# The residual moved to DRAM during the experts, and its SBUF room given to two more weight-chunk places (6 to 8)

## The chip, the cores and the metric

The kernel runs on one core of a Trainium2 chip. The metric is the device time of one execution in microseconds (us); lower is better. The arithmetic is float32 throughout, partly as split pairs of matmuls.

## The reference: one decoder block

512 tokens of width 1024 go through two sub-layers. The first normalises, projects, mixes (eight heads of dilated attention beside four heads of gated linear attention) and projects back. The second is a mixture of 32 experts, four for each token. Both add a gated, normalised result to the residual `x`:

```
x = x + gate1 * rms_norm(hybrid_mixer(h), g_post_mix)     # after this line x is "the residual" of the text
h = rms_norm(x, g_pre_ffn) * (1 + scale2) + shift2
y = moe_ffn(h, router, w_gate_up[32], w_down[32], ...)    # top 4 of 32 experts, clamped SwiGLU
x = x + gate2 * rms_norm(y, g_post_ffn)                   # the residual is read once more, here
```

An expert's weights are 1024 x 2048 (gate and up) and 1024 x 1024 (down), 12 MiB in float32. All 32 are read whatever the routing: 384 MiB.

## The kernel before

**The stages.** Up to about 366 us the mixer runs, then the router: `post(i, ys)` does it for the token tile i (128 tokens, i from 0 to 3). In it the residual of the tile is formed in place in the SBUF tile `X[:, i, :]` (`X` holds 4 x 4 KiB in each of the 128 partitions); it is transposed for the router, squared for its norm, and scaled into `h2`, which goes to DRAM (`h2_d`). From 366 to about 1540 us the experts run, ordered by how many tokens they have. The last 20 us, the tail, add everything up: `acc_d`, in which the experts have summed their outputs in DRAM, is loaded, normalised, added to `X`, and stored.

**Chunks and places.** An expert's weights come in twelve chunks of 1 MiB (the code's "halves"), 384 in all, loaded by `load_half` on SP's DMA queue. Each chunk lands in one of the places of `ring["wr"]`, which are used in turn: 6 places of 8 KiB a partition before the change (five from the pool `wr`, the sixth, `wr6`, opened a little later). The chunks 6 to 8 go once to three extra places, the pool `wx`, which is closed after them. A place is free again when its chunk has been used: for an expert with over 64 tokens in a block, ACT rounds the chunk (`ehi`) and DVE takes the rest (`elo`), in `split_e`, and then the place is free, while PE works from `ehi` and `elo`; for a block of up to 64 tokens ("narrow") PE reads the chunk itself (`gemm_half`; in the profile `bc<-wr` and `ac<-wr`).

**Lists and gathers.** Before an expert starts, `lists` loads its token numbers from a table in DRAM (`li<-tab`, on SP's queue among the chunks), GpSimd gathers the tokens' rows of `h2_d` (`xg<-h_d`, or `xq<-h_d` for narrow blocks), and PE transposes them (`prep`). Bias rows come in small loads (`cb`, `cc`). Outputs are added into `acc_d` by indirect DMAs that GpSimd issues.

**What sets the order.** Nothing is placed by hand from engine to engine. The kernel records its operations in the class `Order`; `S.run()` then lays them out with a cost for each operation, a DMA model and the number of places of each ring, and emits them in that order on each engine. So the number of places does not only bound what is in flight: it changes the order on every engine. In the engines' queues an instruction waits for its semaphores, and what stands behind it waits too. At the end of the experts stands a loop for overflow blocks (`tc.For_i`, line 1628), before which every engine waits for all DMAs.

Of the kernel before, what the change touches and what calls it, by code (L numbers as in the profile page):

```python
# [11 lines left out]
F32 = mybir.dt.float32  # L12
# [5 lines left out]
OP = mybir.AluOpType  # L18
# [4 lines left out]
P, T, NT, D, KD = 128, 512, 4, 1024, 8  # L23
# [7 lines left out]
FIRST, PREP, WX = 8, 9, 3  # L31
# [243 lines left out]
def tile_hybrid_block(ctx, tc, x, c, w_mod, b_mod, g_pre_mix, w_in, w_gate_lr, b_gate, g_gla, w_out,  # L275
                      g_post_mix, g_pre_ffn, router_w, router_b, w_gate_up, b_gate_up, w_down, b_down,
                      g_post_ffn, ca_d, cb_d, tab_d, out, dbg=None):
    nc = tc.nc
# [18 lines left out]
    def close_pool(name):  # L297
# [6 lines left out]
    dp = ctx.enter_context(tc.tile_pool(name="dp", bufs=1, space=DRAM))  # L304
# [12 lines left out]
    S = Order(NB_, 500, ("s", "tr"))  # L317

    ring = {}
# [14 lines left out]
        nc.tensor.matmul(o, l, r, start=start, stop=stop, **kw)  # L334

    h2_d = dp.tile([T, D], F32, name="h2_d")
    acc_d = dp.tile([T + P, D], F32, name="acc_d")
    tab = dp.tile([E * TR, 4], I32, name="tab")
    mrow = dp.tile([8, 512], F32, name="mrow")
# [17 lines left out]
    X = px.tile([P, NT, D], F32, name="X")  # L357
# [55 lines left out]
    def load(q, byt, fn, r=(), w=()):  # L413
        S.op(q, 1.05 if q == "pool" else 0.1, fn, r=r, w=w, byt=byt)
# [44 lines left out]
    for i in range(NT):  # L459
        load("sp", 1 << 19, lambda i=i: nc.sync.dma_start(X[:, i, :], x[i * P:(i + 1) * P]),  # L460
             w=[f"px/Xl{i}", f"px/Xh{i}"])
# [28 lines left out]
    for i in range(NT):  # L490
        S.op("act", _act(1024), lambda i=i: nc.scalar.activation(
            hC[:, 2 * i:2 * i + 2, :].rearrange("p a c -> p (a c)"), X[:, i, :], AF.Square, accum_out=ss1[:, i:i + 1]),
             r=[f"px/Xl{i}", f"px/Xh{i}"], w=[f"ma/C{2 * i}", f"ma/C{2 * i + 1}", f"cp/ss1{i}"])
    cols = [CRG, CQ, CK, CV, CQKG, CVG]
    raws, sp = {}, {}
# [87 lines left out]
    def proj_k(o, n, i, k):  # L583
# [8 lines left out]
         w=["mx/wlr"])  # L592
    for b in range(2):
# [6 lines left out]
                                                      op0=OP.mult), r=["cp/ca"], w=[wlr2])  # L600
    S.op("act", .2, lambda: nc.scalar.activation(wlr2.t[:, :, 0:16], wlr, AF.Copy), r=["mx/wlr"], w=[wlr2])
    S.op("dve", .25, lambda: nc.vector.tensor_sub(wlr2.t[:, :, 16:32], wlr, wlr2.t[:, :, 0:16].bitcast(F32)),
         r=["mx/wlr"], w=[wlr2])
# [378 lines left out]
    def merge(i):  # L982

        S.stream = "mrg"
        oh, ol = buf("oh", [P, KD, P], F32R), buf("ol", [P, KD, P], F32R)
        oTs[i] = oh, ol
        s = slice(i * P, (i + 1) * P)
        S.op("act", _act(512), lambda: nc.scalar.activation(oh.t[:, 0:4, :], qT[:, :, s], AF.Copy), r=[f"mx/q{i}"],
             w=[oh])
        S.op("dve", _dve(512), lambda: nc.vector.tensor_sub(ol.t[:, 0:4, :], qT[:, :, s], oh.t[:, 0:4, :].bitcast(F32)),  # L990
             r=[f"mx/q{i}", oh], w=[ol])
        pt = bank("tr")

        def tr():
            for h in range(4):
                nc.tensor.transpose(pt.t[:, h * P:(h + 1) * P], vg[:, i, h * P:(h + 1) * P], ident)
        S.op("pe", .44, tr, r=[f"px/Xl{i}", f"mx/q{i}", "cp/ca"], w=[pt])
        pv = lambda: pt.t.rearrange("p (h t) -> p h t", h=4)
        S.op("act", _act(512), lambda: nc.scalar.activation(oh.t[:, 4:8, :], pv(), AF.Copy), r=[pt], w=[oh])
        S.op("dve", _dve(512), lambda: nc.vector.tensor_sub(ol.t[:, 4:8, :], pv(), oh.t[:, 4:8, :].bitcast(F32)),  # L1000
             r=[pt, oh], w=[ol])
        load("sp", 1 << 19, lambda: nc.sync.dma_start(X[:, i, :], x[i * P:(i + 1) * P]),
             w=[f"px/Xl{i}", f"px/Xh{i}"])
# [38 lines left out]
    def post(i, ys):  # L1042
        S.stream = "post"
        v = buf("v", [P, 10])
        xi = X[:, i, :]
# [93 lines left out]
             r=xk + [v, rowsA], w=[hk])  # L1139
        S.op("dve", _dve(1024), lambda: nc.vector.tensor_add(h2(), h2(), rv["sh2"]()), r=[rowsB], w=[hk])  # L1140
        load("sp", 1 << 19, lambda: nc.sync.dma_start(h2_d[i * P:(i + 1) * P], h2()), r=[hk] + hold, w=[f"dp/h2{i}"])

    merge(0)
    for i in range(EARLY, NT):
        gla(i)
# [137 lines left out]
    LI, XG, XT, AT, YS, BS, PRE = {}, {}, {}, {}, {}, {}, {}  # L1283
    C = {}

    def load_half(rk, st, h, tag="wr", r=()):
        b = buf(tag, [P, 4, 512])
        load("sp", 1 << 20, lambda: nc.sync.dma_start(
            b.t.rearrange("p (k a) c -> p k (a c)", a=2),
            wsrc(st[0], reg(rk))[h * 256:h * 256 + 256, st[1] * D:st[1] * D + D].rearrange("(k p) c -> p k c", p=P)),  # L1290
            r=rk_(rk) + list(r), w=[b])
        return b
# [3 lines left out]
    def open_wr(name, n):  # L1296
        p = open_pool(name, "right", reuse_waits="tile")
        ring["wr"] = [p.tile([P, 4, 512], F32, name=f"{name}{i}") for i in range(n)] + ring.get("wr", [])
    o1 = S.open("wr", lambda: open_wr("wr", NB_["wr"][0] - 1), after=[c1])
    BB = []  # L1300

    def load_biases():
        for n, (src, w) in enumerate(((b_gate_up, D), (b_down, 512))):
# [3 lines left out]
                load("sp", 32 * 4 * w, lambda b=b, sv=sv, bf_=bf_: nc.sync.dma_start(  # L1307
                    bf_.t[b * E:(b + 1) * E].rearrange("e (s c) -> e s c", c=512), sv[:, :, b // 2, :]), w=[bf_])
            BB.append((bf_, w))
    for n, q in enumerate(halves[:NB_["wr"][0] + WX]):  # L1310
        PRE[q] = load_half(*q, tag="wr" if n < NB_["wr"][0] else "wx", r=["we/w"] if n >= NB_["wr"][0] - 1 else [])
        if n == NB_["wr"][0] - 2:
            cw = S.close(["w2", "md"], lambda: [close_pool(p) for p in ("md", "w2")])

            def open_we():
                open_wr("wr6", 1)
                open_pool("we", "right", reuse_waits="tile")
                open_pool("wx", "right", reuse_waits="tile")
            o2 = S.open("we", open_we, after=[o1, cw])
            S.opened["wx"] = o2  # L1320
            load_biases()
# [272 lines left out]
    consts_a()  # L1594
    prep(E - 1)
    for n, q in enumerate(halves):
        if n == NB_["wr"][0] + WX:
            cx = S.close(["wx"], lambda: close_pool("wx"))

            def open_t2():  # L1600
                p = open_pool("t2", "left", reuse_waits="tile")
                for tag in ("xh", "xl"):
                    ring[tag].insert(0, p.tile([P, KD, P], F32R, name=f"{tag}2"))
            S.open("t2", open_t2, after=[cx, ot])
        for go, r in ahead.get(n, []):
            if go:
                gather(r)
                prep(r)
            else:
                lists(r)  # L1610
        half(*q)
        if n == len(halves) - 6:
            gpb = buf("xg", [P, D])
            load("pool", 1 << 19, lambda: nc.gpsimd.dma_start(gpb.t, mrow_b(None, 3)), w=[gpb])
# [5 lines left out]
    def pair():  # L1620
        t = ring["wr"].pop()
        return [t[:, 2 * h:2 * h + 2, :].rearrange("p a c -> p (a c)") for h in range(2)]
# [29 lines left out]
        S.run()  # L1652


    yp, zp, sq = pair() + pair(), pair() + pair(), pair()[0]
    for i in range(NT):
        nc.sync.dma_start(yp[i], acc_d[i * P:(i + 1) * P])
    nc.scalar.activation(fv[:, 4:5], fv[:, 5:6], AF.Sqrt)
# [6 lines left out]
    for i in range(NT):  # L1665
        z = zp[i]
        nc.scalar.activation(sq, yp[i], AF.Square, accum_out=fv[:, i:i + 1])
        nc.scalar.activation(fv[:, i:i + 1], fv[:, i:i + 1], AF.Sqrt, scale=1.0 / D, bias=fv[:, 5:6])
        nc.vector.reciprocal(fv[:, i:i + 1], fv[:, i:i + 1])
        nc.vector.scalar_tensor_tensor(z, z, fv[:, i:i + 1], X[:, i, :], op0=OP.mult, op1=OP.add)  # L1670
        nc.sync.dma_start(out[i * P:(i + 1) * P], z)
        if i < 2:
            scaled(i + 2, (nc.vector, nc.gpsimd)[i])
# [25 lines left out]
```

## Time and profile before

| what | value |
|---|---|
| time, median of 3 runs (lowest, highest) | 1585.73 us (1584.68, 1587.38) |
| the profiled execution, its own time | 1577.37 us |
| its span, first to last instruction | 1575.5 us |
| busy over the span: PE, DVE, ACT, POOL | 89%, 50%, 38%, 12% |
| moved by DMA | 487.72 MB, 310 GB/s over the span |
| mean granted TensorE clock | 0.969 of full speed |

All rows of the trace come from the profiled execution, which was 8.36 us faster than the median of the three runs; a difference in microseconds is carried over to the median as it is. The DMA share of a stretch is the mean busy share of the 16 DMA engines; in a full stretch it reads slightly above 1.

### The profile page before, as it was taken

To read this page: it belongs to the slowest core of one execution; us is meant where nothing else is said; L and a number is where in the kernel's file an instruction comes from. 1 tells how busy PE (TensorE), PEld (TensorE's weight loads), DVE (VectorE), ACT (ScalarE), POOL (GpSimd) and SP (SyncE) were. 2 spreads that over 40 slices of the span, in tenths; PEclk is the share of its full clock that TensorE was granted. 3 is DMA by queue.
4 is the path that set the end of the run, shared out by engine and by line. 5 is a ranking of instruction groups with operands and counts; after the bars stand their busy time and mean duration, and the time that the engine had idled before them with its cause. 6 is when DMAs were issued, how large, how long until landed. Compare 5 with 4: busy or idle time off the path is not lost.

```text
span 1575.5 us, 17649 instructions
## 1 busy us (share of the span) xinstructions
PE 1409.0 (89%) x6268; PEld 804.4 (51%) x6268; DVE 782.9 (50%) x1164; ACT 596.9 (38%) x798; POOL 183.1 (12%) x161
## 2 busy tenths in 40 slices
PE   3999999987999899899889999999999899999983
PEld 2777666754656544444445553343454443444551
DVE  5787746676765413131356652232565532223663
ACT  4433534433555412122344452223454532224552
POOL 2331001122101000000020020000211101001002
PEclk9999999998999999999989999999999999999997
DMA  9477601176799999989999999999998989989994
GB/s 349 161 265 241 214 1 59 41 260 223 254 398 359 325 366 353 363 308 379 380 344 379 339 385 387 371 369 358 385 394 322 390 305 383 378 330 390 395 357 124
DMA packets 145754, 487.72 MB, mean 310 GB/s; under 512 B 14800, under 2 KB 15328, under 8 KB 145648
## 3 DMA queue, kind: packets, MB, share of 16 engines
q1 hardware_dynamic: 136048, 461.37, 78.4%
q0 software_dynamic: 9616, 25.19, 6.7%
q8 instruction: 51, 0.84, 0.2%
q14 instruction: 39, 0.32, 0.1%
HBM read 467.39 MB, written 19.46 MB: 309 GB/s over the span
## 4 chain that ended last, share of the span: by engine, by line
PE 69%; DMA 13%; DVE 10%; ACT 4%; issue 2%; SPq 0%; POOL 0%; POOLq 0%; DVEq 0%; ACTq 0%
PE ac L334 30%; PE bc L334 21%; PE pj L334 10%; DMA wr<-in_w_gate_up 9%; ACT ehi L1527 3%; DVE elo L1537 3%; PE s L334 2%; DVE mq L478 2%; PE tx L1393 1%; DMA wr<-in_w_down 1%; PE ms L334 1%; PE tx L1408 1%; DMA raw<-in_w_mod 1%; DMA raw<-in_w_in 1%; DVE gl L1499 1%
## 5 line engine op out<-in xcount | busy, mean ns | idle before, releaser
L1537 DVE TENSOR_TENSOR elo<-wr,ehi 128x2048 fp32r<-128x2048 f32 x165 | 377.5, 2290 | 216.7 <-ACT ehi L1527 176.5
L1527 ACT ACTIVATE ehi<-wr 128x2048 fp32r<-128x2048 f32 x165 | 314.0, 1909 | 152.1 <-DMA wr<-in_w_gate_up 109.8
L334 PE MATMUL bc<-wr,xL 128*64 128x512 f32 x1152 | 275.3, 609 | 1.4 <-DMA wr<-in_w_gate_up 1.4
L334 PE MATMUL ac<-ehi,xh 128*128 128x512 f32 (+2 forms) x480 | 170.1, 416 | 26.0 <-ACT ehi L1527 26.0
L334 PE MATMUL ac<-ehi,xl 128*128 128x512 f32 (+2 forms) x480 | 164.3, 404 | 0.0
L334 PE MATMUL ac<-elo,xh 128*128 128x512 f32 (+2 forms) x480 | 141.9, 409 | 6.3 <-DVE elo L1537 6.2
L334 PEld LDWEIGHTS bc<-wr,xL 128*64 128x64 f32 x1152 | 73.6, 137 | 138.0 <-issue 133.7
L334 PE MATMUL bc<-wr,aL 128*64 128x512 f32 x576 | 137.2, 615 | 3.6 <-DMA wr<-in_w_down 3.6
L334 PEld LDWEIGHTS ac<-ehi,xh 128*128 128x128 f32 (+2 forms) x480 | 83.8, 183 | 75.1 <-ACT ehi L1527 37.9
L334 PEld LDWEIGHTS ac<-elo,xh 128*128 128x128 f32 (+2 forms) x480 | 81.5, 179 | 57.2 <-issue 22.7
L1497 DVE TENSOR_SCALAR gu<-bc 128x256 f32<-128x256 f32 x36 | 15.3, 424 | 188.2 <-ACT gl L1495 148.4
L334 PEld LDWEIGHTS ac<-ehi,xl 128*128 128x128 f32 (+2 forms) x480 | 87.5, 182 | 26.6 <-DVE xl L1398 0.2
L334 PE MATMUL ac<-ehi,ah 128*128 128x512 f32 (+2 forms) x240 | 85.0, 416 | 2.7 <-ACT ehi L1527 2.7
L1474 POOL DMA_INDIRECT acc_d<-yL,li x20 | 38.5, 1923 | 399.7 <-ACT yL L1472 353.2
L334 PE MATMUL ac<-ehi,al 128*128 128x512 f32 (+2 forms) x240 | 81.7, 402 | 0.0
L1495 ACT ACTIVATE gl<-bc 128x256 f32<-128x256 f32 x36 | 13.8, 383 | 179.2 <-PE bc L334 163.8
L334 PE MATMUL pj<-whi,hC 128*128 128x512 f32 x192 | 79.7, 415 | 0.9 <-ACT hC L560 0.9
L334 PE MATMUL pj<-whi,hD 128*128 128x512 f32 x192 | 76.2, 397 | 1.7 <-POOL hD L563 1.7
L334 PEld LDWEIGHTS bc<-wr,aL 128*64 128x64 f32 x576 | 38.2, 139 | 77.2 <-issue 72.1
L334 PE MATMUL pj<-wlo,hC 128*128 128x512 f32 x192 | 76.1, 397 | 0.0
L334 PE MATMUL ac<-elo,ah 128*128 128x512 f32 (+2 forms) x240 | 68.0, 396 | 0.0
L478 DVE SCALAR_TENSOR_TENSOR mq<-raw,sil,mq 128x512 f32<-128x512 f32 x74 | 59.2, 800 | 2.1 <-DMA raw<-in_w_mod 0.4
(336 smaller groups left out, 1683.6 us busy)
## 6 DMA issues: line engine op xcount, KB each, us to landing
wr<-in_w_gate_up SPq DMA_DIRECT2D x254, 1024.0 KB, 10.4
wr<-in_w_down SPq DMA_DIRECT2D x127, 1024.0 KB, 10.8
raw<-in_w_mod SPq DMA_DIRECT2D x21, 1024.0 KB, 6.2
raw<-in_w_in SPq DMA_DIRECT2D x12, 1024.0 KB, 10.9
X<-in_x SPq DMA_DIRECT2D x8, 512.0 KB
raw<-in_w_out SPq DMA_DIRECT2D x4, 1024.0 KB
acc_d<-vt SPq DMA_DIRECT2D x5, 512.0 KB, 10.8
wlo<-in_w_mod SPq DMA_DIRECT2D x2, 1024.0 KB
```

The source lines that it names most:

```text
L334: nc.tensor.matmul(o, l, r, start=start, stop=stop, **kw)
L478: f = lambda k=k, s=s: nc.vector.scalar_tensor_tensor(a.t, t.t[:, k, :], s, a.t, op0=OP.mult, op1=OP.add)
L1393: nc.tensor.transpose(pt.t[:, k * m:(k + 1) * m], src(k), ident[:m, :m])
L1408: nc.tensor.transpose(pt.t[:, k * P:(k + 1) * P], src.t[:, k * P:(k + 1) * P], ident)
L1474: load("pool", 1 << 18, lambda: nc.gpsimd.indirect_dma_start(out=acc_2, out_offset=bass.IndirectOffsetOnAxis(ap=li.t[:, 1:2], axis=0), in_ ...
L1495: S.op("act", _acm(256), lambda: nc.scalar.activation(gl.t[:m], gate(), AF.Gelu_apprx_sigmoid), r=[o], w=[gl], table="g")
L1497: S.op("dve", _dvm(256), lambda: nc.vector.tensor_scalar(gu.t[:m], up(), 8.0, -6.0, op0=OP.min, op1=OP.max), r=[o], w=[gu])
L1499: S.op("dve", _dvm(256), lambda: nc.vector.scalar_tensor_tensor(gl.t[:m], gl.t[:m], C["s7"][:m], gu.t[:m], op0=OP.min, op1=OP.mult), r=[gu ...
L1527: S.op("act", _acm(2048), lambda: nc.scalar.activation(hi.t, raw.t, AF.Copy), r=[raw], w=[hi])
L1537: S.op(eng, _dvm(n) if eng == "dve" else .15 + .0021 * n, lambda e=e, c=slice(c0, c1): e.tensor_tensor(lo.t[:, :, c], raw.t[:, :, c], hi.t ...
```

## The change

Four things are edited. (1) `post` also writes the finished residual of its tile to a DRAM tensor `x1_d`, on SP's queue. (2) As chunk 9 comes up, `open_x` puts two places at the head of the ring that are the rows 0 and 1 and the rows 2 and 3 of `X`; it depends on the four writes (`kept`). The ring then has 8 places, and `Order` plans with 8. (3) The chunks 9 and 10 are loaded ahead of everything else recorded for chunk 9, into these two places. (4) In the tail four loads of 512 KiB bring the residual back from `x1_d`, ahead of the four loads of `acc_d`; the last addition reads them in place of `X`.

```
-           "wr": (6, "wr"), ...
+           "wr": (8, "wr"), ...
+    x1_d = dp.tile([T, D], F32, name="x1_d")
@@ post()
         load("sp", 1 << 19, lambda: nc.sync.dma_start(h2_d[i * P:(i + 1) * P], h2()), r=[hk] + hold, w=[f"dp/h2{i}"])
+        kept.append(S.op("sp", 0.1, lambda: nc.sync.dma_start(x1_d[i * P:(i + 1) * P], xi), r=xk, w=[f"dp/x1{i}"],
+                         byt=1 << 19))
@@
+    def open_x():
+        ring["wr"] = [X[:, 2 * n:2 * n + 2].rearrange("p i (k c) -> p (i k) c", c=512) for n in range(2)] + ring["wr"]
@@
-    o1 = S.open("wr", lambda: open_wr("wr", NB_["wr"][0] - 1), after=[c1])
+    o1 = S.open("wr", lambda: open_wr("wr", 5), after=[c1])
+    nwr = 6
@@ the loop over the chunks
-        if n == NB_["wr"][0] + WX:
+        if n == nwr + WX:
+            S.open("xw", open_x, after=kept)
+        if n in (nwr + WX, nwr + WX + 1):
+            PRE[q] = load_half(*q, r=["xw/w"])
+        if n == nwr + WX:
             cx = S.close(["wx"], lambda: close_pool("wx"))
@@ the tail
-    yp, zp, sq = pair() + pair(), pair() + pair(), pair()[0]
+    yp, zp, xp, sq = pair() + pair(), pair() + pair(), pair() + pair(), pair()[0]
+    for i in range(NT):
+        nc.sync.dma_start(xp[i], x1_d[i * P:(i + 1) * P])
     for i in range(NT):
         nc.sync.dma_start(yp[i], acc_d[i * P:(i + 1) * P])
...
-        nc.vector.scalar_tensor_tensor(z, z, fv[:, i:i + 1], X[:, i, :], op0=OP.mult, op1=OP.add)
+        nc.vector.scalar_tensor_tensor(z, z, fv[:, i:i + 1], xp[i], op0=OP.mult, op1=OP.add)
```

Since `Order` lays the program out anew, three places show what moved. The first is SP, where the experts begin (the profile's 366 us). `wr_...` and `X` are the places that chunks go to, `li<-tab` the token lists, `ISA` a register step for an address. Before, two chunks stand ahead of the first list:

```order
L1288 ISA
L1288 DMA wr_2633<-in_w_gate_up 128x2x1024
L1288 DMA wr_2634<-in_w_down 128x2x1024
L1349 DMA li<-tab 128x4
L1355 ISA
L1355 DMA li<-tab 64x4
```

Now, with the first two of them in `X`:

```order
L1296 ISA
L1296 DMA X<-in_w_gate_up 128x2x1024
L1296 DMA X<-in_w_down 128x2x1024
L1296 ISA
L1296 DMA wr_2636<-in_w_gate_up 128x2x1024
L1296 DMA wr_2637<-in_w_down 128x2x1024
L1316 DMA cb<-in_b_gate_up 32x2x512
L1316 DMA cc<-in_b_down 32x512
L1358 DMA li<-tab 128x4
L1364 ISA
L1364 DMA li<-tab 64x4
```

Four chunks and a pair of bias rows now stand ahead of the first list. The last pair of bias rows, which stood between the lists before, comes later still, behind a fifth chunk.

The second place is PE at the same time: the matmuls of the first expert (`ac<-ehi`, `ac<-elo`, and the bias `ac<-bhl`) around the first transposes of gathered rows (`tx<-ca,xq`). Before:

```order
L334 MATMUL ac<-ehi,xl_2975 128x512 x2
L334 MATMUL ac<-elo,xh_2973 128x512 x2
L334 MATMUL ac<-bhl,bs 128x512
L334 MATMUL ac<-elo,xh_2973 128x512 x2
L334 MATMUL ac<-bhl,bs 128x512
L1408 MATMUL tx<-ca,xq 128x128 x4
L334 MATMUL ac<-elo,xh_2973 128x512 x4
```

Now:

```order
L334 MATMUL ac<-elo,xh_2984 128x512 x4
L334 MATMUL ac<-bhl,bs 128x512 x2
L334 MATMUL ac<-ehi,xh_2984 128x512 x2
L334 MATMUL ac<-ehi,xl_2986 128x512 x2
L334 MATMUL ac<-ehi,xh_2984 128x512 x2
L334 MATMUL ac<-ehi,xl_2986 128x512 x2
L334 MATMUL ac<-elo,xh_2984 128x512 x4
L334 MATMUL ac<-ehi,xh_2984 128x512
L334 MATMUL ac<-ehi,xl_2986 128x512
L334 MATMUL ac<-ehi,xh_2984 128x512
L334 MATMUL ac<-ehi,xl_2986 128x512
L1417 MATMUL tx<-ca,xq 128x128 x4
```

Between the first expert's own transposes and `tx<-ca,xq` PE had 58 matmuls before and has 90 now, the bias ones among them.

The third place is SP at the end, behind the overflow loop. Before:

```order
L1628 REGISTER_ALU
L1628 COMPARE_AND_BRANCH
L1628 UNCONDITIONAL_BRANCH
L1657 DMA wr_2635<-acc_d 128x1024 x2
L1657 DMA wr_2634<-acc_d 128x1024 x2
L1671 DMA out<-wr_2633 128x1024 x2
L1671 DMA out<-wr_2785 128x1024 x2
```

Now:

```order
L1641 REGISTER_ALU
L1641 COMPARE_AND_BRANCH
L1641 UNCONDITIONAL_BRANCH
L1670 DMA wr_2640<-x_d 128x1024 x2
L1670 DMA wr_2639<-x_d 128x1024 x2
L1672 DMA wr_2636<-acc_d 128x1024 x2
L1672 DMA X<-acc_d 128x1024 x2
L1686 DMA out<-X 128x1024 x2
L1686 DMA out<-wr_2789 128x1024 x2
```

The four loads of the residual stand behind the loop and ahead of those of `acc_d`.

## Rows read from the trace of the kernel before

**Rows 1.** The page: DMA share (tenths) and rate in 40 equal slices of the span
```profile
DMA  9477601176799999989999999999998989989994
GB/s 349 161 265 241 214 1 59 41 260 223 254 398 359 325 366 353 363 308 379 380 344 379 339 385 387 371 369 358 385 394 322 390 305 383 378 330 390 395 357 124
```
**Rows 2.** Windows by stage: us, busy PE, PEld, DVE, ACT, POOL; clock, DMA share, GB/s
```profile
300.00:366.00 66.00, 55.05 (x282) 36.93 (x280) 46.35 (x155) 23.60 (x48) 13.11 (x25) 0.92 0.58 193
366.00:430.00 64.00, 57.60 (x252) 41.27 (x252) 44.40 (x52) 33.95 (x33) 11.91 (x7) 0.92 0.76 249
430.00:1530.00 1100.00, 1011.18 (x4318) 522.11 (x4317) 468.99 (x488) 401.28 (x434) 97.63 (x61) 0.98 0.99 365
1030.00:1040.00 10.00, 10.00 (x46) 4.54 (x44) 3.27 (x4) 1.14 (x4) 0.00 (x0) 1.00 1.03 413
```
**Rows 3.** Windows of 2 us in 430:1530 with a DMA share under 0.95
```profile
430.00:432.00 2.00, 2.00 (x9) 1.43 (x8) 1.02 (x1) 1.22 (x2) 0.00 (x0) 1.00 0.92 279
...
678.00:680.00 2.00, 2.00 (x11) 1.70 (x12) 1.77 (x5) 0.85 (x3) 0.00 (x0) 1.00 0.57 225
680.00:682.00 2.00, 2.00 (x13) 0.73 (x11) 1.61 (x5) 0.85 (x3) 0.00 (x0) 1.00 0.02 6
682.00:684.00 2.00, 2.00 (x12) 0.69 (x10) 0.63 (x2) 0.38 (x1) 0.00 (x0) 1.00 0.21 31
684.00:686.00 2.00, 2.00 (x12) 0.58 (x8) 0.00 (x0) 0.00 (x0) 0.00 (x0) 1.00 0.82 330
...
1496.00:1498.00 2.00, 2.00 (x10) 1.45 (x9) 0.94 (x1) 1.89 (x1) 0.00 (x0) 1.00 0.89 307
```
**Rows 4.** Waits of SP's queue in 430:1540: us in total, times, longest
```profile
SPq L1288 <- PE bc L334: 434.4, 180, 9.8
SPq L1288 <- DVE elo L1537: 218.2, 74, 14.5
```
**Rows 5.** Waits in 430:1540, ACT's longest on a DMA and PE's two longest
```profile
ACT ehi L1527 <- DMA wr<-in_w_gate_up: 109.4, 42, 7.7
...
PE ac L334 <- ACT ehi L1527: 28.7, 21, 3.2
PE tx L1393 <- DVE gl L1499: 25.0, 17, 3.8
```
**Rows 6.** The chain that ended last, in 430:1540, by line
```profile
by line: PE ac L334 40.2%; PE bc L334 29.5%; DMA wr<-in_w_gate_up 12.6%; ACT ehi L1527 4.3%; DVE elo L1537 3.7%; issue 2.0%; PE tx L1393 1.8%; PE tx L1408 1.7%; DMA wr<-in_w_down 1.1%; DVE gl L1499 1.0%; DVE gu L1497 0.7%; ACT gl L1495 0.5%
```
**Rows 7.** The chain where the experts begin: start us, us, what
```profile
366.65 9.10 DMA wr<-in_w_down
...
378.11 3.64 DMA li<-tab
...
384.00 7.63 DMA xq<-h_d,li
...
411.50 17.00 PE ac L334 x74
```
**Rows 8.** PE's waits in 384:392: us in total, times, longest
```profile
PE tx L1408 <- DMA xq<-h_d,li: 4.0, 1, 4.0
PE ac L334 <- DVE elo L1537: 1.6, 1, 1.6
```
**Rows 9.** DMA issues of the page: times, KB each, median us to landing
```profile
wr<-in_w_gate_up SPq DMA_DIRECT2D x254, 1024.0 KB, 10.4
li<-tab SPq DMA_DIRECT2D x40, 1.0 KB, 10.6
```
**Rows 10.** The timeline of the tail: start us, us, instruction, wait and releaser
```profile
1556.17 1.78 SPq L1657 DMA_DIRECT2D wr<-acc_d  x4
...
1559.35 1.06 ACT L1667 ACTIVATE wr<-wr 128x1024 f32<-128x1024 f32 x1 [1.55 <-DMA wr<-acc_d]
...
1560.69 2.34 POOL L1661 TENSOR_TENSOR wr<-wr,xg 128x1024 f32<-128x1024 f32 x1 [8.71 <-DMA wr<-acc_d]
1564.82 2.62 POOL L1661 TENSOR_TENSOR wr<-wr,xg 128x1024 f32<-128x1024 f32 x1 [1.80 <-DMA wr<-acc_d]
```

More of the change, by code (lines that the diff above doesn't have):

```diff
@@ L1141, in post @@
         load("sp", 1 << 19, lambda: nc.sync.dma_start(h2_d[i * P:(i + 1) * P], h2()), r=[hk] + hold, w=[f"dp/h2{i}"])
+        kept.append(S.op("sp", 0.1, lambda: nc.sync.dma_start(x1_d[i * P:(i + 1) * P], xi), r=xk, w=[f"dp/x1{i}"],
+                         byt=1 << 19))
+    kept = []
     merge(0)
@@ L1309, in load_biases @@
             BB.append((bf_, w))
-    for n, q in enumerate(halves[:NB_["wr"][0] + WX]):
-        PRE[q] = load_half(*q, tag="wr" if n < NB_["wr"][0] else "wx", r=["we/w"] if n >= NB_["wr"][0] - 1 else [])
-        if n == NB_["wr"][0] - 2:
+    for n, q in enumerate(halves[:nwr + WX]):
+        PRE[q] = load_half(*q, tag="wr" if n < nwr else "wx", r=["we/w"] if n >= 5 else [])
+        if n == 4:
             cw = S.close(["w2", "md"], lambda: [close_pool(p) for p in ("md", "w2")])
```

2 rows, old and new, of the table NB_ are left out of this document.

## The prediction, on record before the changed kernel ran

> **What bounds the kernel now.** I read the page's slices first, to see whether the DMA engines ever rest while the experts run. From the tenth slice on they read 8 or 9 tenths, at 305 to 398 GB/s [rows 1]. So the experts are near the limit of the DMA, and PE is near its own: from 430 to 1530 us PE is busy 1011.2 of 1100 us, and the DMA share is 0.99 [rows 2]. A full stretch reads 1.03, at 413 GB/s (1030 to 1040 us, same group). That makes the time in which the DMA engines rest 1100 x (1.03 - 0.99) / 1.03 = 43 us, or 32 us if full is taken as 1.02.
>
> Where they rest I read from windows of 2 us. Of 550 there are 58 with a share under 0.95 (the first, the last and one complete pause in [rows 3]). What they lack of 1.00 adds up to 35 us. They lie in about fifteen pauses, and the longest lacks 4.8 us: 0.43 + 0.98 + 0.79 + 0.18, times 2 us, at 678 to 686 us. In the pause shown PE is busy all the time. So it is not that nothing is wanted: the chunks are all loaded and none is used up fast enough.
>
> SP's waits say the same. It waits 434.4 us in 180 pieces for PE to finish with a place that a narrow block reads, and 218.2 us in 74 pieces for DVE to finish `elo` [rows 4]. Both are waits for a place, and most cost nothing, since several chunks are still under way meanwhile. They cost when all are down.
>
> The other half of the swing is on ACT and PE: ACT waits 109.4 us in 42 pieces for a chunk to land before it can make `ehi`, PE waits 28.7 us for `ehi` and 25.0 us for `gl`, which ACT and DVE bring late [rows 5]. In the chain 12.6% + 1.1% of 1110 us, about 150 us, is a chunk under way [rows 6]. So PE and DMA hold each other up in turn: in heavy stretches DMA rests, in light ones PE starves, and the places are the cushion between the two.
>
> **The change part by part.** The sum is made against the profiled execution, 1577.37 us, and carried over to the median of 1585.73.
>
> *Two more places from 430 us on.* Two chunks are 2 x 1.049 MB; at 365 / 0.99 x 1.03 = 380 GB/s, the phase's rate while it is full [rows 2], they take 5.5 us. A pause of the DMA engines is then put off by 5.5 us of loading, and each of the pauses is shorter than that. Where PE starves between two pauses, the cushion has been emptied and the next pause begins from nothing; where it hasn't, some of the second stays. What DMA doesn't lose, PE and ACT get back as shorter waits for chunks, of which they have more (109.4 us) than DMA has rest (35 us). PE allows it too: it has 1100 - 1011.2 = 89 us of idle time there. Bounds: 0, if something else fills the time, and -43, all the rest there is. I take -25: about seven tenths of the 35 us, since even the longest pause fits into the two places, and less than all of it because PE's idle time isn't all for want of chunks (its waits for `gl` come in part from DVE's own queue) and because the planner's order is new throughout.
>
> *The head start at 366 us.* From 366 to 430 us the share is 0.76 [rows 2], so DMA has 64 x 0.27 / 1.03 = 17 us of rest. Two more chunks are issued into it, worth 5.5 us later. Against that, the first lists stand behind four chunks in place of two. In the chain before, the second chunk lands after 9.10 us, the list after it takes 3.64 us, the gather 7.63 us, and PE then stands 4.0 us [rows 7, 8]. Lists and gather come 5.5 to 8.3 us later now (two or three chunks at 2.76 us). PE however has 90 matmuls ahead of those transposes in place of 58; 32 more at 17.00 us / 74 = 0.23 us [rows 7] are 7.4 us. So PE's stall becomes 4.0 + 5.5 - 7.4 = 2.1 us to 4.0 + 8.3 - 7.4 = 4.9 us: about what it was. What is late next are the bias rows, whose last pair now stands behind the lists and a fifth chunk. I take -3, with bounds of -5.5 (all of the head start kept) and +5 (bias rows and gathers late by two chunks).
>
> *Writing the residual.* Four writes of 0.52 MB fall into 300 to 366 us, where the share is 0.58 [rows 2]; that stretch's rest, 66 x 0.45 / 1.03 = 29 us, covers their 5.5 us. They need no wait of their own on SP, since each stands next to the store of `h2`, which needs later work of the same tile. The new waits before the loads into `X` are for the last of these writes and for readers of `X` that the store of `h2` has waited for already. Cost 0; without that cover, 1.05 MB of the last two tiles, +2.8.
>
> *The tail.* The loads stand behind the loop, after which nothing else is under way, so nothing hides them. Before, the first load of `acc_d` lands 3.2 us after issue (ACT begins at 1559.35), the second is there for POOL at 1560.69, the last at 1564.82 [rows 10]. The first four take the queue 5.1 us at 413 GB/s; by the spacing of the old four, (1564.82 - 1559.35) / 3 = 1.82 us each, 7.3 us. The first `acc_d` tile, from which ACT, DVE and POOL start, comes that much later, and the rest of the tail follows it. I take +6; a list of 1 KB takes 10.6 us to land among the chunks, as long as a chunk [rows 9], so a small or late DMA does not pass earlier ones.
>
> Sum: -25 - 3 + 0 + 6 = -22 us, so 1585.73 - 22 = 1563.7, and 1564 is the forecast. This case's own range goes from all of the 35 us and the whole head start, -35 - 5.5 + 6 = -34.5 or 1551, to somewhat under half of the 35 us, nothing at the head and the dearer tail, -16 + 0 + 7 = -9 or 1577.
>
> **The rivals.**
>
> *The places are not what makes DMA rest (no change).* If the pauses are spent by SP on list loads and register steps, or if the new plan only moves them, no more than the head start stays: -5.5 + 6 = 0, with 2 or 3 us to both sides, 1583 to 1589. For it speaks that lists are issued between chunks throughout; against it that SP's waits are named as PE's and DVE's, 650 us in all [rows 4].
>
> *No bandwidth is left (slower).* When 8 rather than 6 chunks are asked for, each could simply take longer, so that what DMA gains in the pauses it gives back in rate; then only the tail and the later lists are new, +6 + 3 = +9, 1595. It decides from the point where the phase's mean rate cannot rise above 365 GB/s [rows 2]. Against it: a single window moves 413 GB/s [rows 2], so a mean of 365 is not a ceiling. The Trainium skill has a rule that would give this: "DMA: Bandwidth & Descriptors", section "Specifications", puts the HBM limit for one core at about 358 GB/s. The trace disagrees here, since the phase moves 365 GB/s as a mean and 413 in a window; by that rule the two places would be worth nothing.
>
> *Gathers come late (slower).* Lists that queue behind eight chunks land 5.5 us later, and PE's transposes wait. Before, only one gather is on PE's path, the one above [rows 8]. Each further one costs up to 5.5 us, so five of them cancel the 25 us; at seven, 1585.73 - 22 + 38 = 1602. Against it: gathers are started nine chunks before their use, some 28 us at 3.1 us a chunk (366 to 1530 us, by the 375 chunks after the first nine).
>
> *All of the rest is gained.* -43 - 5.5 + 6 = -42, 1543.
>
> **How the numbers follow.** The forecast's case 0.68; all gained 0.04; no change 0.12; no bandwidth 0.09; late gathers 0.07. The range leaves out the last two slower cases and the fastest, 0.20 together, and so runs from 1551 to 1589. Within 0.2% (3.2 us, about what a measurement of this kernel can tell from no change) lies the no-change case, 0.12. Faster are the first two, 0.72; slower the two rivals, 0.16. The forecast's own range is 1551 to 1577.
>
> **What would show it.** Right: from 430 us to the end of the experts the DMA share rises towards 1.02 and the windows under 0.95 fall from 58 to some twenty; ACT's wait for chunks falls by 20 us or more; the last chunk is issued about 28 us earlier; the first `acc_d` tile is there 9 us after the loop in place of 3. Wrong: the share rises but the rate in full windows falls (no bandwidth); PE waits for `xq` or `xg` in many places (late gathers); the pauses stay with SP waiting for the same releases (places not at fault); or the tail takes more than 8 us.

## The result and the profile after

The changed kernel takes 1570.92 us (median of 5, 1568.00 to 1575.41), the kernel before beside it 1584.68 us (median of 5, 1580.25 to 1587.38). The ratio is 0.9914 with an interval of 0.9896 to 0.9931: 13.8 us faster, where 22 us were forecast.

The two profiled executions stand only 2.0 us apart (1577.37 and 1575.41 us): that of before was 7.3 us under its median, that of after 4.5 us over its own. Executions of one kernel scatter by some 10 us, in part with the mean granted clock: of eleven of before that ran beside `best`, the two at 0.966 and 0.967 took 1576.6 and 1576.3 us, the two at 0.957 and 0.958 1586.8 and 1587.8 us; the profiled before had 0.969, the profiled after 0.961. So the medians say how much was won, and the traces where. Windows of after by stage first, which answer to [rows 2]; the columns are the same.

```profile
366.00:430.00 64.00, 52.95 (x223) 35.82 (x223) 38.44 (x57) 28.22 (x29) 8.22 (x9) 0.83 0.67 228
430.00:1530.00 1100.00, 1019.66 (x4390) 534.37 (x4389) 480.48 (x496) 404.82 (x439) 96.17 (x62) 0.98 0.99 367
```

The first stage, which was to gain from the head start, moves less than before (228 GB/s, before 249); that is mostly a later begin, since the last store of `h2` came 2.8 us later in this execution; measured from there, the first 50 MB take as long as before (table below). The long one moves 367 instead of 365 and its share is still 0.99. Now the waits of after in 430 to 1540 us, PE's first, then two of ACT's and two of SP's queue; they answer to [rows 4, 5].

```profile
PE tx L1417 <- DMA xq<-h_d,li: 23.9, 1, 23.9
PE tx L1417 <- DVE gl L1508: 17.3, 12, 1.5
PE ac L334 <- ACT ehi L1536: 15.7, 14, 2.6
PE tx L1402 <- DVE gl L1508: 15.4, 13, 3.5
```

```profile
ACT ehi L1536 <- DMA wr<-in_w_gate_up: 24.1, 8, 5.8
ACT ehi L1536 <- DMA X<-in_w_gate_up: 11.8, 4, 5.8
```

```profile
SPq L1296 <- PE bc L334: 435.2, 173, 8.1
SPq L1296 <- DVE elo L1546: 180.8, 65, 22.2
```

ACT's waits for these chunks fell from 109.4 to 24.1 + 11.8 us, and PE's wait for `ehi` from 28.7 to 15.7 us: the cushion does its work there. New is one wait of PE of 23.9 us for gathered rows, and one of SP's of 22.2 us.

To see where time was won or lost, I added up the bytes moved in windows of 1 us, from the store of the last `h2` tile (358.77 us before, 361.59 after), and asked when 50, 150 and 200 MB had been moved; the end is the tail's first load (1556.17 and 1547.55 us). About 420 MB move in all, the same work in each kernel. These are the stretches in us, for all profiled executions; what each kernel is stands in the next section.

| kernel | places, planned | to 50 MB | 50 to 150 | 150 to 200 | 200 to the end | sum |
|---|---|---|---|---|---|---|
| before | 6, 6 | 159.6 | 285.8 | 135.6 | 616.5 | 1197.4 |
| after | 8, 8 | 159.6 | 274.0 | 147.9 | 604.5 | 1186.0 |
| `parked` | 6, 6 | 156.6 | 286.3 | 135.8 | 618.7 | 1197.4 |
| `tail` | 8, 8 | 160.1 | 272.3 | 148.3 | 603.3 | 1184.0 |
| `seven` | 7, 7 | 159.4 | 273.4 | 142.9 | 612.6 | 1188.3 |
| `plan6` | 8, 6 | 149.6 | 280.8 | 131.7 | 614.9 | 1177.0 |
| `head6` | 6, 6 | 165.5 | 287.6 | 136.4 | 618.4 | 1207.9 |
| `late6` | 6 then 8, 6 | 157.9 | 280.2 | 133.3 | 614.5 | 1185.9 |
| `lists` | 8, 8 | 170.4 | 271.7 | 129.0 | 605.5 | 1176.7 |
| `blists` | 6, 6 | 162.6 | 277.6 | 133.6 | 617.3 | 1191.1 |
| `start` | 8, 8 | 148.5 | 274.9 | 148.3 | 601.9 | 1173.7 |
| `unheld` | 8, 8 | 171.5 | 271.8 | 128.5 | 605.7 | 1177.4 |
| `best6` | 8, 6 | 155.6 | 275.2 | 127.9 | 617.7 | 1176.4 |
| `best` | 8, 8 | 150.9 | 270.1 | 127.9 | 608.0 | 1156.9 |

After gains 12 us between 50 and 150 MB and 12 behind 200 MB, and loses 12 in between. `parked` has the plan and the places of before; where the two differ, by 2 to 3 us, is the scatter of one execution.

**The late gather.** SP's queue in after, 793 to 842 us: start, length, line, DMA.

```profile
793.03 0.99 SPq L1296 DMA_DIRECT2D X<-in_w_gate_up  x2
797.10 0.37 SPq L1296 DMA_DIRECT2D wr<-in_w_gate_up  x1
797.71 0.34 SPq L1358 DMA_DIRECT2D li<-tab  x1
798.27 0.50 SPq L1364 DMA_DIRECT2D li<-tab  x1
799.61 0.34 SPq L1358 DMA_DIRECT2D li<-tab  x1
800.78 0.48 SPq L1364 DMA_DIRECT2D li<-tab  x1
803.12 0.36 SPq L1358 DMA_DIRECT2D li<-tab  x1
805.83 0.48 SPq L1364 DMA_DIRECT2D li<-tab  x1
810.04 2.65 SPq L1296 DMA_DIRECT2D wr<-in_w_gate_up  x2
812.89 3.43 SPq L1364 DMA_DIRECT2D li<-tab  x4
838.72 3.70 SPq L1296 DMA_DIRECT2D wr<-in_w_gate_up  x3
```

Ten loads of 1 KB go out from 797.7 to 816.3 us, in a row with chunks. PE, the gathers of POOL that follow the first lists, and the windows around the pause:

```profile
798.71 0.51 PE L334 MATMUL bc<-bhl,bL 128*128 128x512 f32 x1
823.08 1.09 PE L1417 MATMUL tx<-ca,xq 128*128 128x128 f32 x4 [23.87 <-DMA xq<-h_d,li]
```

```profile
812.61 0.97 POOL L1379 DMA_INDIRECT xg<-h_d,li  x1 [10.85 <-DMA li<-tab]
813.89 0.99 POOL L1379 DMA_INDIRECT xq<-h_d,li  x1 [0.31 <-issue]
```

```profile
800.00:820.00 20.00, 0.00 (x0) 0.00 (x0) 0.34 (x2) 1.73 (x1) 4.45 (x4) 0.61 1.01 335
820.00:840.00 20.00, 16.92 (x69) 9.46 (x70) 6.15 (x12) 6.18 (x7) 2.84 (x3) 0.80 0.32 86
```

PE's other work is over at 799.22 us, 1.5 us after the first list goes out. That list is down some 15 us after its issue, right behind the chunk of 797.10, and the gather that PE needs (813.89) takes 9 us more, to 823.08. Before, 25.6 us lie between the first list of the row and the same transposes, and PE has work until then:

```profile
784.49 0.49 SPq L1355 DMA_DIRECT2D li<-tab  x1
810.07 1.09 PE L1408 MATMUL tx<-ca,xq 128*128 128x128 f32 x4
```

So the lists come too late because they are issued late against PE's work; their way is little longer (14.9 us from the first list to the first gather, before 11.5). SP also holds some of them back. Its DMAs take eight semaphores in turn (no exception among the 531 of the trace), and each waits until the one issued eight before it has landed. With eight chunks under way, a list can so wait for a chunk that it has nothing to do with. SP's waits from 796 to 818 us show two such lists:

```profile
SPq L1364 <- DMA X<-in_w_gate_up: 2.1, 1, 2.1
...
SPq L1358 <- DMA wr<-in_w_gate_up: 1.1, 1, 1.1
```

These two waits don't lengthen the stall, since those lists (803.12 and 805.83 us) land with the first ones, less than 1 us behind them.

PE's stall costs DMA nothing at first (share 1.01): the places fill up. Then they are full, and DMA rests from 822 to 840 us (share 0.32), while SP waits its 22.2 us for `elo`.

**The start.** SP's queue in after, where the experts begin:

```profile
370.27 0.83 SPq L1296 DMA_DIRECT2D wr<-in_w_down  x1
371.14 0.59 SPq L1316 DMA_DIRECT2D cb<-in_b_gate_up  x1
...
372.75 0.35 SPq L1358 DMA_DIRECT2D li<-tab  x1
...
386.12 0.40 SPq L1296 DMA_DIRECT2D wr<-in_w_down  x1
386.57 0.67 SPq L1316 DMA_DIRECT2D cb<-in_b_gate_up  x1
...
390.12 0.52 SPq L1364 DMA_DIRECT2D li<-tab  x1
```

The last pair of bias rows goes out at 386.57 us, 17.7 us after the first chunk of 368.92 (before 6.1 us), the last of the first lists at 390.12, 21.2 us after it (before 13.3 us). What idles for the bias tile `cb` in 366 to 430 us, by tile, in after and then in before:

```profile
  DMA cb<-in_b_gate_up: 6.9, 1
  DVE cb L1578: 5.5, 1
```

```profile
  DMA cb<-in_b_gate_up: 5.4, 1
  DVE cb L1569: 1.4, 1
```

DVE stands 6.9 us for the bias rows, and ACT 5.5 us for DVE; behind them in their queues stand `ehi` and `elo` of the first expert, and PE's wait for `elo` grows from 1.6 us [rows 8] to 6.1 us. The wait of 4.0 us for `xq` is gone in exchange. The stall comes back on DMA a little later: from 396 to 436 us its engines rest 14.0 us (windows of 2 us, what they lack of a share of 1.00), before 9.0.

**The tail.** The timeline of after:

```profile
1547.55 1.77 SPq L1670 DMA_DIRECT2D wr<-x_d  x4
...
1549.36 0.99 SPq L1672 DMA_DIRECT2D wr<-acc_d  x2
...
1557.11 1.06 ACT L1682 ACTIVATE wr<-wr 128x1024 f32<-128x1024 f32 x1 [7.94 <-DMA wr<-acc_d]
```

ACT begins 9.6 us after the first load, where it took 3.2 us before [rows 10]; to the end of the span it is 25.95 us, before 19.33: +6.6.

### The profile page after: what moved, and what is told of

It reads as the page before. It is cut to its first block, busy times and chain, and to the rows that moved or that the text cites. A ratio compares the mean times of both kernels' runs of the same rounds, so it can differ in the third digit from the quotient of the medians.

```text
span 1573.5 us, 17660 instructions
## 1 busy us (share of the span) xinstructions
PE 1405.3 (89%) x6268; PEld 807.4 (51%) x6268; DVE 782.5 (50%) x1164; ACT 592.7 (38%) x798; POOL 176.4 (11%) x161
## 5 line engine op out<-in xcount | busy, mean ns | idle before, releaser
L1546 DVE TENSOR_TENSOR elo<-wr,ehi 128x2048 fp32r<-128x2048 f32 x121 | 276.2, 2290 | 144.2 <-ACT ehi L1536 109.0
L1536 ACT ACTIVATE ehi<-wr 128x2048 fp32r<-128x2048 f32 x121 | 229.5, 1909 | 62.3 <-DMA wr<-in_w_gate_up 24.1
L334 PE MATMUL bc<-wr,xL 128*64 128x512 f32 x888 | 212.6, 608 | 0.0
L1546 DVE TENSOR_TENSOR elo<-X,ehi 128x2048 fp32r<-128x2048 f32 x44 | 100.5, 2289 | 41.2 <-ACT ehi L1536 30.7
L334 PEld LDWEIGHTS bc<-wr,xL 128*64 128x64 f32 x888 | 57.0, 137 | 106.5 <-issue 104.8
L334 PE MATMUL bc<-wr,aL 128*64 128x512 f32 x440 | 102.6, 600 | 0.0
L1536 ACT ACTIVATE ehi<-X 128x2048 fp32r<-128x2048 f32 x44 | 84.0, 1911 | 20.9 <-DMA X<-in_w_gate_up 11.8
L1504 ACT ACTIVATE gl<-bc 128x256 f32<-128x256 f32 x36 | 13.8, 382 | 196.7 <-PE bc L334 187.5
L1483 POOL DMA_INDIRECT acc_d<-yL,li x20 | 35.3, 1767 | 385.3 <-ACT yL L1481 328.7
```

Source lines behind the costliest of these rows:

```text
L1483: load("pool", 1 << 18, lambda: nc.gpsimd.indirect_dma_start(out=acc_2, out_offset=bass.IndirectOffsetOnAxis(ap=li.t[:, 1:2], axis=0), in_ ...
L1504: S.op("act", _acm(256), lambda: nc.scalar.activation(gl.t[:m], gate(), AF.Gelu_apprx_sigmoid), r=[o], w=[gl], table="g")
L1536: S.op("act", _acm(2048), lambda: nc.scalar.activation(hi.t, raw.t, AF.Copy), r=[raw], w=[hi])
L1546: S.op(eng, _dvm(n) if eng == "dve" else .15 + .0021 * n, lambda e=e, c=slice(c0, c1): e.tensor_tensor(lo.t[:, :, c], raw.t[:, :, c], hi.t ...
```

## The experiments

In all of them the computation is whole; they differ in places, order and buffers. Ratios are to the kernel before, run beside them on the same chip.

**`parked` and `tail`: what the tail costs.** `parked` is the kernel before with the residual written to `x1_d` and read back into `X` in the tail, no more places. `tail` is the change with the eight loads of the tail in turn:

```
     for i in range(NT):
-        nc.sync.dma_start(xp[i], x1_d[i * P:(i + 1) * P])
-    for i in range(NT):
         nc.sync.dma_start(yp[i], acc_d[i * P:(i + 1) * P])
+        nc.sync.dma_start(xp[i], x1_d[i * P:(i + 1) * P])
```

> One part of the change alone: the residual is written to DRAM in post and read back in the tail (into X itself, four loads ahead of those of acc_d), with 6 places as before. If writing is covered and only the tail pays (the prediction's terms), the first chunk of the experts is still issued near 366 us, the tail is 6 to 7 us longer and the time is 1591. If the writes hold up the router as well (in the changed kernel's profile that issue came at 368.9 us), it is 2 to 3 us more, 1594.

> The changed kernel with one edit: in the tail each load of acc_d is issued ahead of the load of the residual of the same tile, where all four of the residual came first. The plan ahead of the tail stays as it is. If the tail's extra 6.6 us come from waiting for the first acc_d tile, that tile is there about 3 us after issue and 4 to 5 us are given back: 1566. If they come from the bytes as such (2 MB more before the last tile can be finished), nothing or 1 us is given back: 1570. The profile also shows whether the one wait of 23.9 us for a gather at 823 us belongs to the plan: it should be there again, 15 to 25 us long.

`parked`: 1584.81 us, 1.0018 [0.9998, 1.0037]; `tail`: 1568.39 us, 0.9904 [0.9882, 0.9927]. In its profile `parked` needs 6.7 us more behind the loop than before, and `tail` 1.7 us more (21.06 against 19.33 us). Of the 6.6 us, 4.9 so come from waiting for the first `acc_d` tile, and the rest goes with the bytes. The medians put the cost in `parked` at 2 to 3 us, and its interval, -0.3 to +5.9 us, doesn't exclude nothing; the forecast of 1591 missed, and why the medians show less than the profile stays open. PE's wait for `xq` stays in `tail` (23.8 us) and is not there in `parked`: it comes with the eight places and their plan.

**`seven` and `plan6`: places against plan.** `seven` opens one of the two places in `X` and plans with 7. `plan6` has the 8 places, but `Order` lays the program out for 6:

```
-           "wr": (8, "wr"), ...
+           "wr": (6, "wr"), ...        # plan6
```

> One more place instead of two (X rows 0 and 1), planned with 7. Theory: with 8 places SP has as many chunks under way as it can have DMAs (each of its DMAs waits for the one eight before it), so list loads go out one for each chunk that lands, a gather comes late and PE stands 24 us; with 7 places one DMA is left for lists, no wait for a gather is over 8 us, and the time is as good as with 8 or better, 1566 to 1572. Rival: places are worth what they are, the late gather only stands where PE would have waited anyway; then 7 places give half of what 8 give in the experts (about 20 us before the tail's cost), 1584.7 - 10 + 6.6 = 1581.

> The changed kernel with 8 places, but planned with 6, so that the order of lists and chunks on SP and the order on PE are nearly those of before, with lists about two chunks earlier in SP's order than in the changed kernel. Theory (late lists cost the rest of the gain): the wait for the gather shrinks to 10 us or less, the DMA pause behind it too, and the time is 1556 to 1564. Rival (the plan's order doesn't matter, or the order for 8 places is the better one for 8): 1569 to 1575.

`seven`: 1576.45 us, 0.9948 [0.9928, 0.9968], with a wait for `xq` of 12.7 us; about half of the gain for half of the places. Both forecasts missed: it lies between 1572 and 1581, and the wait is longer than the 8 us of the first. `plan6`: 1567.57 us, 0.9901 [0.9878, 0.9923]. The wait for `xq` is gone (its longest is 1.3 us from 430 us on), and from 150 to 200 MB it is 16 us faster than after. But from 200 MB to the end it takes 614.9 us, hardly less than before. The forecast of 1556 to 1564 failed: with the late gather went what the plan for 8 had won elsewhere.

**`head6` and `late6`: head start against room.** `head6` gives the chunks 9 and 10 the places in `X` once, and stays at 6 otherwise; `late6` is `plan6` with the two places joining at chunk 60 (`joined[0]` is the load of chunk 59).

```
-        ring["wr"] = [X[...] for n in range(2)] + ring["wr"]
+        ring["xx"] = [X[...] for n in range(2)]          # head6; chunks 9 and 10 take tag "xx"
...
-        if n == nwr + WX:
-            S.open("xw", open_x, after=kept)
+        if n == JOIN:                                    # late6; JOIN = 60
+            S.open("xw", open_x, after=kept + joined[0].ops)
```

> The head start alone: the ring stays at six places and is planned with six, and chunks 9 and 10 go once to the two places in X (the residual is written, and read back into X in the tail). Theory that eight chunks in flight raise the rate all along (windows with a share over 0.95: 386 GB/s in the run planned with six, 381 before): the head start is worth no more than its 5.5 us and the tail takes 2 to 6 of them back, so 1579 to 1585 beside 1583 for before. Rival, that the two chunks loaded ahead at 366 us are the gain and are carried to the end: 1567 to 1571, as the run planned with six.

> The eight places without the head start: planned with six, and the two places in X join the ring only at chunk 60, some 150 us into the experts. Theory of the rate: 1567 to 1573, the gain of the run planned with six (15 us) less about a tenth of it for the first 60 of 384 chunks and up to 3 us for the head start. Rival, the head start: 1580 to 1585. Halves of both: about 1576.

`late6`: 1571.50 us, 0.9921 [0.9891, 0.9952], as its first theory had it: the room helps without the head start. `head6`: 1596.05 us, 1.0070 [1.0045, 1.0096], 11 us worse than that theory's upper end: four chunks ahead of the first lists are no small gain but a loss. It takes 165.5 us to the first 50 MB, `parked` 156.6. DVE waits 10.0 us for the bias rows in `head6`, 3.9 us in `parked`, and from 396 to 436 us DMA rests 15.0 us, 7.6 in `parked`. PE's wait from 366 to 440 us, in `head6` (4.0 us in `parked`):

```profile
PE ac L334 <- DVE elo L1546: 9.7, 2, 7.7
```

**`lists` and `blists`: more list buffers.** The lists at 797 us stand in a row because the plan loads a list when one of 8 `li` buffers comes free. `lists` is the change with 16 (16 bytes a partition each), `blists` the kernel before with 16.

```
-           "li": (8, "tk"), ...
+           "li": (16, "tk"), ...
```

> The change as made, with sixteen li buffers in place of eight, so that no token list has to wait for a buffer and ten lists no longer stand in one row among eight chunks at 798 us. Theory of the late gather: PE's wait of 23.9 us for xq and the pause of the DMA engines behind it (13.8 us) go, and the rate of the other stretches (376 GB/s) holds throughout, so 8 to 14 us less than the change: 1557 to 1563. Rival, that the wait stands where PE and DMA lose that time anyway, as the run planned with six suggests: 1566 to 1571.

> The kernel before, with sixteen li buffers, nothing else. If late lists are a matter of eight chunks in flight, nothing is won here: 1581 to 1586. If the li buffers hold back the order at six places too, 1570 to 1578.

`lists`: 1560.24 us, 0.9849 [0.9813, 0.9885], 10 us better than the change. The wait for `xq` is gone, and 150 to 200 MB take 129.0 us in place of 147.9. `blists`: 1571.39 us, 0.9924 [0.9896, 0.9951]: the buffers held back the order at six places as well, where my theory had them hold back only eight. There the gain lies at 50 to 150 MB. So how much of the 10 us is the late gather's the medians don't tell; that it cost 16 to 20 us where it happened rests on the stretches of the profiles.

**`start`, `best`, `best6`, `unheld`: mends together.** `start` is the change with the chunks 11 and 12 planned behind the bias rows and the first eleven lists (and every list behind the bias rows). `best` adds sixteen `li` buffers and the tail of `tail`; `best6` is `best` without the first mend and planned with 6; `unheld` is `best` without the first mend.

```
+        if n in (nwr + WX + 2, nwr + WX + 3):
+            PRE[q] = load_half(*q)
+            S.ops[-1].deps += first          # the loads of bias rows and of the first lists
...
+                for i in new:                # the list loads just recorded
+                    S.ops[i].deps += first[:8]
```

> The change as made (8 places, planned with 8), but chunks 11 and 12 go out behind the first eleven lists and the bias rows, so that two chunks stand ahead of the first list, as before, and not four. Theory that the head start costs time (the run with the head start alone had lost 7 us by the first 50 MB of the experts, and the change itself had not gained by then): 7 to 11 us less than the change, 1558 to 1563. Rival, that this loss at the beginning is made up later by the two places: 1567 to 1571.

> All three mends together: 8 places planned with 8, sixteen li buffers, chunks 11 and 12 behind the first lists and bias rows, the tail's loads of the residual and of the sums in turn. If the losses add up (late lists 10 us, head start 7 to 11, tail 2 to 6): 1541 to 1551. If PE, busy 1089 us in the experts, bounds them from here: not under 1550.

> As the last, but planned with six places, which by itself puts two chunks ahead of the lists. If the plan has to know of the eight places to use them, slower than the last by 5 us or more, 1550 to 1560; if the places work by being there, the same within 3 us.

> The version with all three mends, less one: four chunks again stand ahead of the first lists and bias rows (8 places planned with 8, sixteen li buffers, the tail's loads in turn). If the head start costs what the beginning of the profiled runs lost, some 10 us or more (18 us by the first 50 MB, between the run with sixteen buffers and the one with all mends), 1552 to 1560. If most of that is made up later, as the small gain of the run with that mend alone allows (3 us), 1543 to 1548.

| kernel | median, us | ratio |
|---|---|---|
| `start` | 1565.47 | 0.9894 [0.9866, 0.9922] |
| `best` | 1541.58 | 0.9747 [0.9722, 0.9773] |
| `best6` | 1561.69 | 0.9873 [0.9846, 0.9899] |
| `unheld` | 1559.54 | 0.9814 [0.9786, 0.9842] |

`best` is 39.6 us faster than before, and as fast as the sum of the mends had it; 1541.58 us is under the 1550 that PE's busy time would have set, so PE is not the bound yet. `best` against `unheld` prices the four chunks ahead of the bias rows and lists: 0.0067 of 1585, or 11 us; DVE waits 13.0 us for the bias rows in `unheld` and not at all in `best`, and DMA rests 16.9 and 3.0 us from 396 to 436 us. `start` against the change shows only 0.002, 3 us, with intervals that overlap; its first 50 MB are 11 us faster, though, so for that pair the size stays open, and the median lies between the two forecasts. `best6`, just above its forecast of 1550 to 1560, is 20 us slower than `best`, half of it behind 200 MB, where it takes as long as six places do: there the places are worth little unless the plan knows of them. SP in `best` at the start:

```profile
367.62 0.59 SPq L1316 DMA_DIRECT2D cb<-in_b_gate_up  x1
...
369.59 0.66 SPq L1316 DMA_DIRECT2D cb<-in_b_gate_up  x1
...
380.61 4.76 SPq L1366 DMA_DIRECT2D li<-tab  x6
385.57 0.43 SPq L1296 DMA_DIRECT2D wr<-in_w_gate_up  x1
```

The last bias rows go out 3 us after the first chunk (366.61 us), in after 18; PE's wait for `elo` there is 2.7 us. What `best` makes of the stretch in which the change had its late gather, and behind it the same stretch of the change (367 GB/s before):

```profile
700.00:970.00 270.00, 255.02 (x1108) 136.74 (x1106) 128.03 (x130) 110.68 (x118) 34.25 (x19) 0.99 1.03 386
```

```profile
700.00:970.00 270.00, 237.04 (x1020) 131.67 (x1017) 121.37 (x117) 105.41 (x106) 28.03 (x18) 0.94 0.96 351
```

## Why the prediction was right in sign and 7 us off

**Two more places from 430 us on: right mechanism, mis-sized at -25.** From 50 MB to the end of the experts the profiled pair shows 1037.9 and 1026.4 us, -11.5. The profiled before ran at a higher clock; `parked`, six places at 0.962, takes 1040.8 us, 14.4 more than after (0.961) and 16.9 more than `tail` (0.962). So the term is 11 to 17 us in place of 25. Without the late gather the two places are worth nearly the forecast: with sixteen `li` buffers in both kernels (both at 0.963), `blists` takes 1028.5 us for this part and `lists` 1006.2, -22.3. So the term stood near its size, and one stall of PE, which the sum had at nothing, took 5 to 11 us of it back by this comparison. By medians, `best` against `blists` is 0.0177 of 1583, 28 us, for the two places, what they win at the start and what the mended tail still costs.

A new plan moves the time by itself: `blists` gains 12 us by medians with the places of before. With the plan for six held, the two places are worth 13.4 us of this part (`plan6` 1027.4 us against `parked`).

The step that "each of the pauses is shorter than that" and so fits into two places was too good. Of 550 windows of 2 us, 54 still have a share under 0.95 and lack 36.6 us. 13.8 of that are the pause behind the late gather, and 5.0 come after the last chunk (1516 us); the other 17.8 stand against 35.2 before. So half of the rest went; counted the same way, `lists` has 18.1 and `best` 15.7, `blists` 31.1. The longest old pause, which lacked 4.8 us, is still there and lacks 5.0; its middle in after:

```profile
676.00:678.00 2.00, 1.62 (x9) 1.08 (x8) 1.77 (x5) 0.96 (x3) 0.00 (x0) 1.00 0.83 330
678.00:680.00 2.00, 2.00 (x12) 1.27 (x12) 1.58 (x5) 0.95 (x4) 0.00 (x0) 1.00 0.09 35
680.00:682.00 2.00, 2.00 (x12) 0.64 (x10) 1.17 (x3) 0.20 (x2) 0.00 (x0) 1.00 0.03 8
682.00:684.00 2.00, 2.00 (x10) 0.63 (x10) 0.42 (x1) 0.35 (x1) 0.00 (x0) 1.00 0.62 145
```

The other part of the gain was not in the sum: windows with a share of 0.95 and more move 384.0 GB/s as a mean, before 380.9. (In `lists` and `blists` it is 382.8 and 382.4, so that this comes from the places is not shown.) Where both places and plan are 8 the rest halves; in `plan6` it is 32.9 us (48.5 less 15.6 after the last chunk), nearly that of before. That a larger cushion is simply full when the next heavy stretch begins would explain it, but is only argued.

**Head start: -3 forecast, 0 measured (159.6 us to 50 MB in both; +3 against `parked`).** The bounds held, and what was named as late next, the bias rows, was late. But the gain and the loss were both larger than thought: with bias rows and lists ahead of the chunks 11 and 12 the eight places win 9 to 11 us there (`best`, `start`), and with four chunks in front they lose all of it, and more with sixteen buffers (`lists`, `unheld`). The working counted the gather and PE's 90 matmuls, and not that DVE and ACT stand for the bias rows with `elo` and `ehi` behind them. The runs moved bias rows and lists together, so how much each of them costs is not shown apart.

**Writing the residual: 0, right as far as can be told.** The last `h2` store of after is 2.8 us later than before, but `lists`, with the same instructions up to there, has it at 358.84 us, against 358.77.

**The tail: +6 forecast, +6.6 in the profile.** By medians it is smaller: 2 to 3 us for `parked`; what loading in turn gives back is 1.6 us from after to `tail` and 5.5 from `lists` to `unheld` by their ratios, both with intervals that overlap.

**The rivals.** Late gathers came once. Their price was wrong: 23.9 us of PE's time and 16 to 20 us of the stretch (147.9 against 131.7, 129.0 and 127.9), not the 5.5 us by which two more chunks delay a list, and "seven" of them were not needed. The rival's argument, a lead of nine chunks, looked at the gather's place among the chunks and not at the list, which the plan loads late for want of a buffer and which needs 25 us with its gather. No bandwidth left is refuted: `best` moves 386 GB/s as a mean over 270 us. By the Trainium skill's figure ("DMA: Bandwidth & Descriptors", section "Specifications", about 358 GB/s) the two places were to be worth nothing; with the kernel on one core, the measurement decides against it. No change and all of the rest gained were both missed by the medians.

**The signs.** ACT's waits, the tail and the missing fall of the rate came as foretold. Not so the windows under 0.95 (54, not twenty), the share (0.99, not 1.02), and the last chunk, issued 12.1 us earlier (1515.88 and 1527.94 us), not 28. The slices of [rows 1] were read two too early: DMA is at 8 or 9 tenths from the twelfth to the last but one, and nothing in the sum hangs on that.

## What to carry to other kernels

More room for a stream of large loads also lengthens the queue in which the small loads stand that other engines wait for, and lets those engines reach the wait sooner: look for the smallest transfer on the same queue (here 1 KB lists and bias rows), ask when it is issued against the work that needs it, and put it ahead of the large ones or give it buffers enough to be loaded early. A rival that needs many small delays to matter should also be priced as one large one: a stall of the bound engine long enough to fill every place. Where a planner decides the order, test places and plan apart, since here, with lists and start in order, the places without the plan (`best6`) stood 8 us from six places (`blists`) and 20 us from places with plan (`best`).

## What the runs showed of the hardware that was not expected

PE's stall is paid by DMA later: in 800 to 820 us PE is idle and the share 1.01, and in 820 to 840 us PE works and the share is 0.32. The granted clock also fell while PE stood: PE's last matmul ends at 799.22 us, windows of 2 us in after show full speed up to 804, 0.57 from 804 to 806 and 0.50 (the lower level, 1.2 GHz) from there on. It is still 0.50 as PE returns at 823.08, and 0.96 in the window from 828 us.

```profile
804.00:806.00 2.00, 0.00 (x0) 0.00 (x0) 0.00 (x0) 0.00 (x0) 0.00 (x0) 0.57 1.02 354
...
822.00:824.00 2.00, 0.92 (x5) 0.95 (x6) 0.69 (x4) 0.00 (x0) 0.96 (x1) 0.50 0.27 62
...
828.00:830.00 2.00, 2.00 (x10) 0.54 (x8) 0.34 (x2) 0.36 (x1) 0.00 (x0) 0.96 0.63 234
```

And a core's DMA can move more than the phase's mean before had shown as a matter of course: 386 GB/s over 270 us in `best`, with eight chunks under way and a share of 1.03.
